# Four feed-forwards that open with two tiles of plain products, in a transformer program on one Trainium2 core

## The chip, the core and the metric

The program runs on one core of one Trainium2 chip. Times are device microseconds (us) of one execution. PE is TensorE (matmul), DVE VectorE, ACT ScalarE, POOL GpSimd, SP the engine that issues the loads.

## What is computed

Two blocks over 512 tokens of 1,024 channels, in float32. The first has two layers, each a feed-forward, a mixer (SSD and S5; then chunked attention and pooling) and another feed-forward; the second is a hybrid mixer and one feed-forward between layer norms. The five feed-forwards are called ffn0 to ffn4 here.

```python
def _swiglu(h, w_gate, w_up, w_down):
    return (jax.nn.silu(h @ w_gate) * (h @ w_up)) @ w_down
...
    for layer in range(DEPTH):
        h = _rmsnorm(x, ffn1_norm[layer])
        x = x + 0.5 * _swiglu(h, ffn1_w_gate[layer], ffn1_w_up[layer], ffn1_w_down[layer])
        h = _rmsnorm(x, mix_norm[layer])
...
        x = x + mixed.astype(x.dtype)
        h = _rmsnorm(x, ffn2_norm[layer])
        x = x + 0.5 * _swiglu(h, ffn2_w_gate[layer], ffn2_w_up[layer], ffn2_w_down[layer])
...
        x = layer_norm(alpha * x + mix, ln1_g[l], ln1_b[l])
        ff = swiglu_ffn(x, w_ffn_gate[l], w_ffn_up[l], w_ffn_down[l])
```

## The kernel before

x lies in SBUF with channels on partitions: eight tiles x[d] of 128 channels by 512 tokens, taken in the order DORD = 0, 4, 1, 5, 2, 6, 3, 7. A float32 operand is split in two parts of a type that PE takes at full rate: ACT copies the high part (xh, wh, th, aH), DVE subtracts it from the operand for the low part (xl, wl, tl, aL). A product of two operands is three matmuls: high by high, low by high, high by low.

A feed-forward has 2,816 = 22 tiles of 128 inner channels f, in parts of 7, 8 and 7. For each f gate and up are multiplied over the eight d, then silu and the product make a; after a part its down products add to x (stt, L280). ffn1 to ffn3 are normed: the gain is multiplied in with the split, and rstd (one over the root of the mean square) is multiplied in behind the products. rstd needs products with ones over the sums of squares (ssum, sq), a chain of operations on four columns on DVE (small), and a product with csts that spreads it over the partitions.

**Quad.** A tile f is done by `quad` (L512). Gate and up for two token halves and two halves of d would be eight block products; with sums of weights and sums of operands seven do. That is 7 × 4 × 3 = 84 matmuls of 256 columns. `wsums` (L572) makes the sums of weights sa and sb on POOL; `prep_t` (L457) makes the sums of operands: for k = 0 to 3, from x[k] and x[k+4], four differences (tt), and splits them into seven slots of th and tl. Four of the slots lie in the room of xh and xl, three in th1 and tl1.

In ffn1, ffn2 and ffn3 every tile is a quad, so `prep_t(k)` runs as soon as x[k] and x[k+4] are there: in `even` and `odd` (L971, L1362) behind the mixer's last products, in `epi_res` (L718) behind ffn1's down products. ffn0 opens with plain products: in part 0 each f is 48 matmuls of 512 columns, and its sums are made after that part.

**ffn4's opening.** The layer norm before it goes by token halves. `ahead` (in the main function) first issues the right half's sums; `quad_a` multiplies the two block products that need the left half alone, for four tiles; between them `ln_cols_b`, `ln_rows` and `ln_apply` (L1877, L1895, L1907) normalise the right half, and `prep_t1` makes the sums. `quad_b` does the other five block products of these tiles.

The tile scheduler orders each engine's instructions by priority; weight splits have `high_priority`, and inside `pe_order` PE keeps the order of the code. PSUM tiles are named by tags (mm, aux, acc, p12) with a number of buffers each. A load is 512 KB per gate or up weight, in five buffers `raw`.

Of the kernel before, what the change touches and what calls it, by code (L numbers as in the profile page):

```python
# [9 lines left out]
F32 = mybir.dt.float32  # L10
# [7 lines left out]
T = 512  # L18
# [20 lines left out]
T4 = 5  # L39
AHEAD = 4  # L40
# [210 lines left out]
class Net:  # L251
# [164 lines left out]
    def prep(self, k, gain, steps=3):  # L416
        x = self.x[:, k]
        if gain is None:
            self.hilo(self.xh[:, k], self.xl[:, k], x)
            return  # L420
        if steps & 1:
            gc = self.vec(gain, k)
            self.act(self.xh[:, k], x, AF.Copy, scale=gc)
            self.stt(self.xl[:, k], x, gc, self.xh[:, k].bitcast(F32), ALU.mult, ALU.subtract)
# [3 lines left out]
        self.act(sq, x, AF.Square)  # L428
# [11 lines left out]

    def t_open(self):
        self.tx = ExitStack()
        self.tpool = self.tx.enter_context(self.tc.tile_pool(name="tx", bufs=1, side="right", reuse_waits="tile"))
        b = lambda t: t.rearrange("p (s k) (u t) -> p (s k u t)", s=4, u=2).rearrange("p (s k t) -> p s k t", s=4, k=4)
        self.th0, self.tl0 = b(self.xh), b(self.xl)
        self.th1 = self.tpool.tile([128, 3, 4, H], F32R, name="th1")
        self.tl1 = self.tpool.tile([128, 3, 4, H], F32R, name="tl1")
        self.TH = [self.th0[:, s] for s in range(4)] + [self.th1[:, s] for s in range(3)]
        self.TL = [self.tl0[:, s] for s in range(4)] + [self.tl1[:, s] for s in range(3)]
# [7 lines left out]
    def prep_t(self, k, gain, stats=True):  # L457

        G = self.nc.gpsimd
# [17 lines left out]
        if gain is not None and stats:  # L477
            sq = self.t4([2, T], "sq2")
            self.act(sq[:, 0], self.x[:, k], AF.Square)
            self.act(sq[:, 1], self.x[:, k + 4], AF.Square)  # L480
            if k == 0:
                self.ssum = self.sp.tile([128, T], F32, name="ssum", tag="ssum", bufs=1)
                self.add(self.ssum, sq[:, 0], sq[:, 1], self.on("sst"))
            elif k < 3:
                self.add(self.ssum, self.ssum, sq[:, 0], self.on("sst"))
                self.add(self.ssum, self.ssum, sq[:, 1], self.on("sst"))
            else:
                self.sums = [self.ssum, sq[:, 0], sq[:, 1]]

    def prep_t0(self, d):  # L490

        if d == 0:
            b = lambda t: t.rearrange("p (s k) (u t) -> p (s k u t)", s=4, u=2).rearrange("p (s k t) -> p s k t", s=4, k=4)
            self.th0, self.tl0 = b(self.xh), b(self.xl)
        s, k = d // 4, d % 4
        self.hilo(self.th0[:, s, k], self.tl0[:, s, k], self.x[:, d, 0:H])

    def prep_t1(self, k):

        G = self.nc.gpsimd  # L500
# [34 lines left out]
    def quad_a(self, src):  # L535

        t = self.wp.tile([128, 8, 128], F32, name="raw", tag="raw", bufs=5)
        self.nc.sync.dma_start(t, src)
        with self.tc.high_priority(offset=PRIO):
            h, l = self.wsplit(t)  # L540
        ps = self.psum("p12")
        for k in range(4):
            for s in range(2):
                o = ps[:, H * s:H * s + H]
                j = 4 * s + k
                self.mm(o, h[:, j], self.TH[s][:, k], k + s == 0, False)
                self.mm(o, h[:, j], self.TL[s][:, k], False, False)
                self.mm(o, l[:, j], self.TH[s][:, k], False, k + s == 4)
        return ps

    def quad_b(self, sp, src1, src2, by_k):

        r = []
        for s in (src1, src2):
            t = self.wp.tile([128, 8, 128], F32, name="raw", tag="raw", bufs=5)
            self.nc.sync.dma_start(t, s)
            r.append(t)
        r1, r2 = r
        with self.tc.high_priority(offset=PRIO):
            wa, wb, w2 = self.wsums(sp, r1, r2)  # L560
# [1628 lines left out]
```

## Time and profile before

| | before |
|---|---|
| three runs | 2833.72, 2842.39, 2843.31 us; median 2842.39 |
| profiled execution | 2844.66 us; span 2842.9 us |
| busy: PE, DVE, ACT, POOL | 2747.3, 1921.9, 1608.5, 966.1 us |

Busy time is an average over stages with different limits. The timeline gives start, duration, engine, line, operation and tile, then the idle time before it and what released it; durations of neighbours overlap a little, since an engine starts on the next while the last result is written. f and d of a product are told by its place.

### The profile page before, as it was taken

How to read it: one execution, taken by the hardware profiler on the slowest of the kernel's cores; microseconds unless marked ns; L12 is line 12 of the kernel's file. 1: busy time of each engine (PE TensorE's matmuls, PEld its weight loads, DVE VectorE, ACT ScalarE, POOL GpSimd, SP SyncE). 2: the span in 40 equal slices, each digit the busy share in tenths (PEclk: the TensorE clock that was granted, in tenths of full speed). 3: DMA queues.
4: the chain of work that ended last, by engine and by line, in shares of the span. 5: the costliest groups of instructions: out<-in, count | busy, mean ns of one | idle time of the engine just before them, and what ended most of it. 6: DMA issues, size and time to landing. Idle time of an engine off the chain costs nothing. (4 is left out here: it accounts for less than half of the span.)

```text
span 2842.9 us, 44877 instructions
## 1 busy us (share of the span) xinstructions
PE 2747.3 (97%) x16940; PEld 2453.4 (86%) x16940; DVE 1921.9 (68%) x3472; ACT 1608.5 (57%) x2593; POOL 966.1 (34%) x849
## 2 busy tenths in 40 slices
PE   8899999989999999999998999999999999889997
PEld 6798988879999899998777999987888788889997
DVE  7885856688576886766556867675886434765665
ACT  5375834647676766766434767653443543466674
POOL 5752414235344353442002534421000102544352
PEclk9999998999999999999999999999999899899998
DMA  5333354203332233324221333234323133132321
GB/s 181 114 108 101 107 156 124 84 30 100 108 113 89 86 96 106 115 89 127 72 67 33 99 107 117 89 110 137 95 86 103 55 101 114 53 104 97 119 86 56
DMA packets 106760, 279.58 MB, mean 98 GB/s; under 512 B 31984, under 2 KB 34672, under 8 KB 106544
## 3 DMA queue, kind: packets, MB, share of 16 engines
q1 hardware_dynamic: 106400, 276.54, 31.2%
q8 instruction: 133, 2.18, 0.3%
q14 instruction: 83, 0.68, 0.1%
q10 hardware_dynamic: 144, 0.18, 0.0%
HBM read 258.54 MB, written 11.85 MB: 95 GB/s over the span
## 5 line engine op out<-in xcount | busy, mean ns | idle before, releaser
L290 ACT ACTIVATE wh<-raw 128x1024 fp32r<-128x1024 f32 (+2 forms) x467 | 439.0, 944 | 608.0 <-PE mm L293 456.9
L293 PE MATMUL mm<-xh,wh 128*128 128x512 f32 (+1 forms) x1592 | 556.4, 350 | 18.3 <-ACT wh L290 7.0
L293 PE MATMUL mm<-xh,wl 128*128 128x512 f32 (+1 forms) x1592 | 546.6, 343 | 4.9 <-DVE wl L265 4.9
L293 PE MATMUL mm<-xl,wh 128*128 128x512 f32 (+1 forms) x1592 | 547.2, 344 | 3.9 <-DVE xl L280 2.3
L265 DVE TENSOR_TENSOR wl<-raw,wcopy 128x512 fp32r<-128x512 f32 (+1 forms) x410 | 257.1, 659 | 212.4 <-PE mm L293 92.7
L293 PEld LDWEIGHTS mm<-xh,wh 128*128 128x128 f32 x1592 | 309.5, 194 | 59.7 <-issue 11.5
L265 POOL TENSOR_TENSOR sa<-raw 128x512 f32<-128x512 f32 x103 | 139.5, 1354 | 617.6 <-DVE wl L265 266.0
L293 PEld LDWEIGHTS mm<-xh,wl 128*128 128x128 f32 x1592 | 309.2, 194 | 39.7 <-DVE wl L265 6.2
L293 PEld LDWEIGHTS mm<-xl,wh 128*128 128x128 f32 x1592 | 309.4, 194 | 36.4 <-DVE xl L280 4.9
L265 DVE TENSOR_TENSOR wl<-raw,wh 128x1024 fp32r<-128x1024 f32 (+1 forms) x159 | 205.4, 1293 | 124.6 <-ACT wh L290 118.5
L293 PE MATMUL aux<-xh,wh 128*128 128x256 f32 (+1 forms) x880 | 262.3, 298 | 5.2 <-DVE x L265 3.3
L293 PE MATMUL aux<-xh,wl 128*128 128x256 f32 (+1 forms) x880 | 261.8, 297 | 2.9 <-DVE wl L265 2.9
L293 PE MATMUL aux<-xl,wh 128*128 128x256 f32 (+1 forms) x880 | 261.2, 297 | 3.2 <-DVE xl L265 3.2
L293 PE MATMUL mm<-th,wh 128*128 128x256 f32 x824 | 232.7, 282 | 5.1 <-DVE x L265 3.3
L290 ACT ACTIVATE wcopy<-raw 128x512 fp32r<-128x512 f32 (+1 forms) x410 | 229.2, 573 | 8.3 <-DVE wl L265 7.7
L293 PE MATMUL mm<-tl,wh 128*128 128x256 f32 x824 | 231.5, 281 | 0.3 <-DVE tl L265 0.2
L293 PE MATMUL mm<-th,wl 128*128 128x256 f32 x824 | 230.8, 280 | 0.0
L293 PEld LDWEIGHTS aux<-xh,wh 128*128 128x128 f32 x880 | 174.5, 198 | 8.4 <-DVE x L265 3.6
L293 PEld LDWEIGHTS aux<-xh,wl 128*128 128x128 f32 x880 | 173.8, 198 | 6.0 <-DVE wl L265 3.5
L293 PEld LDWEIGHTS aux<-xl,wh 128*128 128x128 f32 x880 | 173.5, 197 | 6.1 <-DVE xl L265 3.7
L265 DVE TENSOR_TENSOR wl<-sa,wcopy 128x512 fp32r<-128x512 f32 x186 | 126.3, 684 | 76.2 <-ACT wcopy L290 44.9
L265 POOL TENSOR_TENSOR wl<-raw,wh 128x512 fp32r<-128x512 f32 x103 | 140.4, 1363 | 108.9 <-ACT wh L290 108.9
(491 smaller groups left out, 7081.4 us busy)
## 6 DMA issues: line engine op xcount, KB each, us to landing
raw<-in_gu SPq DMA_DIRECT2D x224, 512.0 KB, 3.8
raw<-in_wd SPq DMA_DIRECT2D x80, 448.0 KB, 3.3
raw<-in_hy_in SPq DMA_DIRECT2D x60, 512.0 KB, 3.8
raw<-in_wd SPq DMA_DIRECT2D x40, 512.0 KB, 3.5
raw<-in_ev_in SPq DMA_DIRECT2D x17, 512.0 KB, 3.9
raw<-in_od_in SPq DMA_DIRECT2D x16, 512.0 KB, 3.8
sw<-qk SPq DMA_DIRECT2D x48, 128.0 KB, 2.3
raw<-in_ev_out SPq DMA_DIRECT2D x8, 512.0 KB, 3.8
```

The lines of the kernel that those rows point to most:

```text
L265: (eng or self.nc.vector).tensor_tensor(out=out, in0=a, in1=b, op=op)
L290: self.nc.scalar.activation(out, a, func, **kw)
L293: self.nc.tensor.matmul(ps, a, b, start=start, stop=stop)
```

## The change

- **ffn1, ffn2, ffn3** (`open_plain`): f = 0 and 1 are plain products, 48 matmuls of 512 columns each. Tile 0 has d outside and gate and up inside, tile 1 gate then up. The sums of squares come after tile 0, the spread of rstd after tile 1's gate. `prep_t` is called after tile 0's products.
- **ffn4** (`open_halves`): f = 0 and 1 by token halves, four PSUM tiles at once for the left half, then three for the right and the fourth behind: 96 matmuls of 256 columns a tile. The layer norm of the right half comes as hooks between the left half's d; `prep_u` splits one d of one half.
- xh and xl are now written at once in the quad's slots (`slot`), by `prep(..., slots=True)`, so the plain products read them in two pieces of 256 columns (`direct`), in ffn0's part 0 too. `prep_t` makes the four sums alone; th1 and tl1 hold four slots, not three; the buffers t4 are 3, not 5.
- `quad_a`, `quad_b`, `prep_t0` and `prep_t1` go. Squares are summed on POOL to two tensors, not three, before the products with ones.

```diff
-T4 = 5
-AHEAD = 4
+T4 = 3
+ND = 2
...
-        self.th1 = self.tpool.tile([128, 3, 4, H], F32R, name="th1")
+        self.th1 = self.tpool.tile([128, 4, 4, H], F32R, name="th1")
...
+    def slot(self, t, d):
+
+        q = self.quarters(t)
+        return q[:, 0:4:3, d] if d < 4 else q[:, 1:3, d - 4]
...
         tt = self.t4([4, H], "tt")
-        self.hilo(self.th0[:, 0, k], self.tl0[:, 0, k], aL)
         self.sub(tt[:, 0], aR, aL)
-        self.hilo(self.th0[:, 3, k], self.tl0[:, 3, k], tt[:, 0])
-        self.hilo(self.th0[:, 1:3, k], self.tl0[:, 1:3, k], b.rearrange("p (u t) -> p u t", u=2))
+        self.sub(tt[:, 2], bR, aR, self.on("tt"))
         self.sub(tt[:, 1], bR, tt[:, 0])
-        self.sub(tt[:, 2], bR, aR, self.on("tt"))
         self.sub(tt[:, 3], bL, tt[:, 1])
-        self.hilo(self.th1[:, :, k], self.tl1[:, :, k], tt[:, 1:4])
...
+        self.hilo(self.th1[:, :, k], self.tl1[:, :, k], tt)
...
+    def direct(self, ps, w, d, lo=0, hi=2):
+
+        o = ps if hi - lo == 2 else ps[:, H * lo:H * hi]
+        ah, al = self.slot(self.xh, d)[:, lo:hi], self.slot(self.xl, d)[:, lo:hi]
+        h, l = w
+        self.mm(o, h[:, d], ah, d == DORD[0], False)
+        self.mm(o, h[:, d], al, False, False)
+        self.mm(o, l[:, d], ah, False, d == DORD[7])
...
+    def open_plain(self, i, gain):
+
+        A = self.A
+        out = []
+        with self.pe_order():
+            for f in range(ND):
+                w = [self.weights(A["gu"][i, f, :, s]) for s in range(2)]
+                ps = [self.psum("mm"), self.psum("aux")]
+                for d, s in ([(d, s) for d in DORD for s in range(2)] if f == 0 else [(d, s) for s in range(2) for d in DORD]):
+                    self.direct(ps[s], w[s], d)
+                    if f == 1 and d == DORD[7] and s == 0:
+                        self.rms_b("acc")
+                if f == 0:
+                    self.rms_a("acc")
+                out.append(ps)
+                if f == 0:
+                    for k in range(4):
+                        self.prep_t(k, gain)
+        return out
+
+    def open_halves(self, i, hooks):
+
+        A = self.A
+        with self.pe_order():
+            hooks[-1]()
+            w = [self.weights(A["gu"][i, f, :, s]) for f in range(2) for s in range(2)]
+            ps = [self.psum(t) for t in ("mm", "aux") * 2]
+            for n, d in enumerate(DORD):
+                for t in range(4):
+                    self.direct(ps[t], w[t], d, 0, 1)
+                if n in hooks:
+                    hooks[n]()
+            for d in DORD:
+                for t in range(3):
+                    self.direct(ps[t], w[t], d, 1, 2)
+            for d in DORD:
+                self.direct(ps[3], w[3], d, 1, 2)
+        for k in range(4):
+            self.prep_t(k, None)
+        return [ps[0:2], ps[2:4]]
...
-            if last and not ffn_next:
-                self.prep(d, gain)
-            elif last and d >= 4:
-                self.prep_t(d - 4, gain)
+            if last:
+                self.prep(d, gain, slots=ffn_next)
...
-            self.prep_t(d2, gain)
+                self.prep(d, gain, slots=True)
...
+            hooks = {-1: lambda: self.ln_cols_a(1, "acc"), 1: cols, 5: rows}
+            self.ffn(4, None, epi, tail=self.ln_tail, hooks=hooks)
```

**DVE ahead of and in ffn3's opening.** x_72 is x; the additions of mm_ tiles are those of the mixer's last products, and the twelfth row is that of x[7]. Before, x[6] and x[3] are added in the first and the seventh row:

```order
L265 TENSOR_TENSOR x_72<-x_72,mm_16206 128x512
L265 TENSOR_TENSOR xl_74<-xg_16165,xh_73 128x2x256
L265 TENSOR_TENSOR tt_16223<-xg_16220 128x256
L265 TENSOR_TENSOR tl1_16075<-tt_16168,th1_16074 128x3x256
L265 TENSOR_TENSOR xl_74<-xg_16220,xh_73 128x256
L265 TENSOR_TENSOR tt_16223<-xg_16220,tt_16223 128x256
L265 TENSOR_TENSOR x_72<-x_72,mm_16247 128x512
L265 TENSOR_TENSOR tt_16223<-xg_16220,tt_16223 128x256
L265 TENSOR_TENSOR xl_74<-tt_16223,xh_73 128x256
L265 TENSOR_TENSOR xl_74<-xg_16220,xh_73 128x2x256
L265 TENSOR_TENSOR tt_16278<-xg_16275 128x256
L265 TENSOR_TENSOR x_72<-x_72,mm_16261 128x512
```

Of the change, the twelve rows up to x[7], with x[6] and x[3] in the fourth and the ninth; wl_16004 is the split of tile 0's up weight, wl_16124 that of tile 1's gate weight:

```order
L265 TENSOR_TENSOR wl_16004<-raw_16001,wh_16003 128x1024
L280 SCALAR_TENSOR_TENSOR xl_74<-x_72,vecs_75,xh_73 128x2x256
L265 TENSOR_TENSOR tt_16094<-xg_16091,tt_16094 128x256
L265 TENSOR_TENSOR x_72<-x_72,mm_15918 128x512
L265 TENSOR_TENSOR tl1_15985<-tt_16084,th1_15984 128x4x256
L265 TENSOR_TENSOR tt_16094<-xg_16091,tt_16094 128x256
L280 SCALAR_TENSOR_TENSOR xl_74<-x_72,vecs_75,xh_73 128x2x256
L265 TENSOR_TENSOR wl_16124<-raw_16121,wh_16123 128x1024
L265 TENSOR_TENSOR x_72<-x_72,mm_15943 128x512
L280 SCALAR_TENSOR_TENSOR xl_74<-x_72,vecs_75,xh_73 128x2x256
L265 TENSOR_TENSOR tt_16104<-xg_16101 128x256
L265 TENSOR_TENSOR x_72<-x_72,mm_15962 128x512
```

The quarter-wide xl of the sums are gone; whole xl (128x2x256), splits of both tiles' weights and the four-wide tl1 stand between the additions now, and xl of d = 3 and 7 still come behind x[7].

**PE at the start of ffn3.** Before, with mm_16261 the last product of the mixer:

```order
L293 MATMUL mm_16261<-yl_14490,wh_16243 128x512
L293 MATMUL mm_16261<-yh_14489,wl_16244 128x512
L293 MATMUL mm_16328<-xh_73,wh_16306 128x256
L293 MATMUL mm_16328<-xl_74,wh_16306 128x256
L293 MATMUL mm_16328<-xh_73,wl_16307 128x256
```

Of the change, with mm_15962 that last product, and mm_16007 and aux_16008 the gate and up tiles of f = 0:

```order
L293 MATMUL mm_15962<-yh_14223,wl_15940 128x512
L293 MATMUL mm_16007<-xh_73,wh_15997 128x512
L293 MATMUL mm_16007<-xl_74,wh_15997 128x512
L293 MATMUL mm_16007<-xh_73,wl_15998 128x512
L293 MATMUL aux_16008<-xh_73,wh_16003 128x512
L293 MATMUL aux_16008<-xl_74,wh_16003 128x512
L293 MATMUL aux_16008<-xh_73,wl_16004 128x512
L293 MATMUL mm_16007<-xh_73,wh_15997 128x512
```

The first products of 256 columns read one slot and one weight; now three of 512 for gate are followed at once by three for up. The PSUM buffer of aux_16008 is that of mm_15962, which the addition of x[7] reads.

**DVE at the end of ffn4's opening.** Before, from the last two tl1 on (pu is the first step of tile 0's sums):

```order
L265 TENSOR_TENSOR tl1_24553<-tt_24707,th1_24552 128x3x256
L265 TENSOR_TENSOR tl1_24553<-tt_24724,th1_24552 128x3x256
L265 TENSOR_TENSOR pu_24797<-pu_24797,mm_24822 128x256
L265 TENSOR_TENSOR wl_24916<-sb_24906,wh_24915 128x1024
L265 TENSOR_TENSOR pu_24797<-pu_24797,mm_24822 128x256
L265 TENSOR_TENSOR aux_24821<-pu_24797,aux_24821 128x256
L265 TENSOR_TENSOR acc_24823<-pu_24797 128x256
```

Of the change, from the last two xl on; aux_24203 and aux_24205 are f = 0's and f = 1's up tiles, wl_24528 is f = 2's:

```order
L265 TENSOR_TENSOR xl_74<-x_72,xh_73 128x256 x2
L265 TENSOR_TENSOR tt_24498<-x_72,tt_24498 128x256
L265 TENSOR_TENSOR tl1_24163<-tt_24491,th1_24162 128x4x256
L265 TENSOR_TENSOR tt_24498<-x_72,tt_24498 128x256
L265 TENSOR_TENSOR aux_24203<-aux_24203,u_24505 128x512
L265 TENSOR_TENSOR aux_24205<-aux_24205,u_24512 128x512
L265 TENSOR_TENSOR tl1_24163<-tt_24498,th1_24162 128x4x256
L265 TENSOR_TENSOR aL_24509<-aux_24203,aH_24508 128x512
L265 TENSOR_TENSOR aL_24516<-aux_24205,aH_24515 128x512
L265 TENSOR_TENSOR wl_24528<-raw_24523,wcopy_24530 128x512
L265 TENSOR_TENSOR wl_24528<-raw_24523,wcopy_24533 128x512
```

The last sums stand behind the last xl, and f = 2's weight split behind the epilogues of both plain tiles and the last tl1.

## Rows read from the trace of the kernel before

**Rows 1.** The page, parts 1 and 2: PE's total, and its clock by slice.

```profile
PE 2747.3 (97%) x16940; PEld 2453.4 (86%) x16940; DVE 1921.9 (68%) x3472; ACT 1608.5 (57%) x2593; POOL 966.1 (34%) x849
...
PEclk9999998999999999999999999999999899899998
```

**Rows 2.** Windows (stretch; length, busy us by engine, clock, DMA, GB/s): four openings, steady state.

```profile
625.95:664.57 38.62, 30.57 (x198) 29.50 (x196) 35.56 (x47) 22.65 (x35) 27.15 (x19) 0.78 0.21 68
984.45:1020.55 36.10, 31.55 (x198) 30.90 (x197) 28.48 (x42) 18.95 (x29) 22.26 (x16) 0.76 0.24 74
1549.00:1587.55 38.55, 31.29 (x198) 30.48 (x198) 34.09 (x46) 20.80 (x31) 26.76 (x18) 0.73 0.17 55
2445.70:2530.30 84.60, 64.89 (x442) 61.65 (x441) 64.03 (x120) 45.22 (x76) 47.12 (x38) 0.84 0.21 68
2600.00:2660.00 60.00, 60.00 (x506) 60.00 (x505) 45.77 (x84) 48.81 (x78) 36.46 (x30) 1.00 0.33 107
```

**Rows 3.** The chain that ended last (start, us, what): two quads, ffn4.

```profile
2651.50 5.71 PE mm L293 x48
...
2661.51 5.71 PE mm L293 x48
```

**Rows 4.** Waits of PE in 1549 to 1588: total us, times, longest.

```profile
PE mm L293 <- DVE x L265: 3.6, 1, 3.6
PE aux L293 <- DVE x L265: 3.3, 1, 3.3
```

**Rows 5.** Waits of PE in 2445 to 2531, ffn4's opening.

```profile
PE mm L293 <- DVE x L265: 3.3, 1, 3.3
PE aux L293 <- DVE xl L265: 3.2, 2, 2.0
```

**Rows 6.** Windows: from the first to the last addition before ffn3.

```profile
1534.52:1557.90 23.38, 17.18 (x74) 13.84 (x72) 23.38 (x29) 15.47 (x28) 15.06 (x11) 0.87 0.00 0
```

**Rows 7.** Timeline of DVE (start, us, operation) ahead of ffn3: additions to x.

```profile
1534.52 1.89 DVE L265 TENSOR_TENSOR x<-x,mm 128x512 f32<-128x512 f32 x3 [0.82 <-PE mm L293]
...
1557.90 0.68 DVE L265 TENSOR_TENSOR x<-x,mm 128x512 f32<-128x512 f32 x1
```

**Rows 8.** Timeline of DVE, ffn1's opening: split, xl, x[7], scalars of rstd.

```profile
613.24 1.22 DVE L265 TENSOR_TENSOR wl<-raw,wh 128x1024 fp32r<-128x1024 f32 x1
...
630.32 1.49 DVE L265 TENSOR_TENSOR xl<-tt,xh 128x256 fp32r<-128x256 f32 x1
...
634.82 0.68 DVE L265 TENSOR_TENSOR x<-x,mm 128x512 f32<-128x512 f32 x1
...
641.64 0.16 DVE L287 TENSOR_SCALAR small<-aux 128x4 f32<-128x4 f32 x1 [0.27 <-PE aux L293]
...
649.29 1.41 DVE L280 SCALAR_TENSOR_TENSOR small<-small 128x4 f32<-128x4 f32 x2
```

**Rows 9.** Timeline of DVE, ffn4's opening: the last xl.

```profile
2480.69 0.41 DVE L265 TENSOR_TENSOR xl<-tt,xh 128x256 fp32r<-128x256 f32 x1
```

**Rows 10.** Timeline of POOL beside the xl at 630.32.

```profile
630.07 1.45 POOL L265 TENSOR_TENSOR sa<-raw 128x512 f32<-128x512 f32 x1
```

**Rows 11.** Timeline of PE in ffn0's plain products, the first and the last of 19.

```profile
59.76 0.39 PE L293 MATMUL aux<-xl,wh 128*128 128x512 f32 x1
...
63.84 0.39 PE L293 MATMUL aux<-xl,wh 128*128 128x512 f32 x1
```

**Rows 12.** Timeline of PE in ffn1's opening, two products of 256 columns.

```profile
632.07 0.41 PE L293 MATMUL aux<-xh,wh 128*128 128x256 f32 x1
632.28 0.41 PE L293 MATMUL aux<-xl,wh 128*128 128x256 f32 x1
```

**Rows 13.** Timeline of PE, ffn4: a wait, and the first product of f=5.

```profile
2518.65 0.58 PE L293 MATMUL mm<-xh,wl 128*128 128x256 f32 x1 [2.66 <-DVE wl L265]
...
2530.30 0.28 PE L293 MATMUL aux<-xh,wh 128*128 128x256 f32 x1
```

More of the change, by code (lines that the diff above doesn't have):

```diff
@@ L477, in prep_t @@
[L477 to L488, printed above, removed]
@@ L591, in wsplit, with rms_a, rms_b @@
         return h, l
-    def rms_a(self):
+    def rms_a(self, tag="aux"):
         v = self.small(4)
-        self.ts(v, self.col_sums([self.sums]), 1.0 / 1024, EPS, ALU.mult, ALU.add)
+        self.ts(v, self.col_sums([self.sums], tag=tag), 1.0 / 1024, EPS, ALU.mult, ALU.add)
         self.rstd_c = self.rsqrt(v, 4)
-    def rms_b(self):
+    def rms_b(self, tag="aux"):
         self.rstd = self.sp.tile([128, T], F32, name="rstd", tag="rstd", bufs=1)
-        self.act(self.rstd, self.rows(self.rstd_c), AF.Copy, scale=RS)
+        self.act(self.rstd, self.rows(self.rstd_c, tag), AF.Copy, scale=RS)
     def rms(self):
@@ L604, in rms @@
         self.rstd_rows([self.sums], 1.0 / 1024, EPS, self.rstd)
-    def ffn(self, i, normed, epi, bg=None, first=None, tail=None, ahead=None):
+    def open_plain(self, i, gain):
[16 more added lines that the diff above has]
+        return out
@@ L608, in ffn @@
+    def ffn(self, i, gain, epi, bg=None, tail=None, hooks=None):
         nc, A = self.nc, self.A
         G = nc.gpsimd
-        if ahead:
-            self.spare = 0
-            self.psum_open(p12=AHEAD, aux=2, mm=1, acc=1)
-        elif not first:
-            self.lend()
-        with self.tc.tile_pool(name="ffn", bufs=1, reuse_waits="tile") as fp:
-            pend = []
-            if ahead:
-                order = self.pe_order()
-                order.__enter__()
-                ahead(-1)
-                for f in range(AHEAD):
-                    pend.append(self.quad_a(A["gu"][i, f, :, 0]))
-                    ahead(f)
+        first = bg is not None
+        normed = gain is not None
+        if not first:
+            self.t_open()
+            if hooks:
+                self.spare = 0
+                self.psum_open(mm=2, aux=2, acc=4)
+            else:
+                self.lend()
+        with self.tc.tile_pool(name="ffn", bufs=1, reuse_waits="tile") as fp:
+            if not first:
+                plain = self.open_halves(i, hooks) if hooks else self.open_plain(i, gain)
@@ L626, in ffn @@
                 for f in range(f0, f0 + nf):
-                    if ahead and f == AHEAD:
-                        order.__exit__(None, None, None)
+                    if hooks and f == ND:
                         self.lend()
@@ L631, in ffn @@
                         self.spare = 2 if f >= NDIR else 1
-                    if first and part == 0:
-                        ps = []
-                        for s in range(2):
-                            w = self.weights(A["gu"][i, f, :, s] if f + s else None)
-                            p = self.psum("mm" if s == 0 else F0T)
-                            self.mm3(p, w, 0, 8, self.xh, self.xl)
-                            ps.append(p)
-                        if f == 0:
-                            self.rms()
+                    if first and part == 0 or f < ND:
+                        if first:
+                            ps = []
+                            for s in range(2):
+                                w = self.weights(A["gu"][i, f, :, s] if f + s else None)
+                                ps.append(self.psum("mm" if s == 0 else F0T))
+                                for d in DORD:
+                                    self.direct(ps[s], w, d)
+                            if f == 0:
+                                self.rms()
+                        else:
+                            ps = plain[f]
```

182 lines of the change are left out of this document (59 added, 123 removed).

## The prediction

> **What bounds the kernel now.** I read the page first: TensorE (PE) is busy for 97% of the span and its clock is at or near full in nearly every slice [rows 1]. So the end is set by PE's own work and by the few places where PE stands. The windows over the four openings of ffn1, ffn2, ffn3 and ffn4, each from PE's first product of the feed-forward to the first of a later tile, come second [rows 2]. The stretch 2600 to 2660 is the steady state: PE busy for all of 60.00 us at clock 1.00. The openings are not like that. In 38.62, 36.10 and 38.55 us PE does two tiles in ffn1, ffn2, ffn3, and in 84.60 us five tiles in ffn4, at a mean clock of 0.73 to 0.84, which lies between the two levels of 1.2 and 2.4 GHz. A steady tile takes 10.01 us, from 2651.50 to 2661.51 in the chain [rows 3]. Two would be 20.0 us and five 50.1. So the openings hold 18.6 + 16.1 + 18.5 + 34.5 = 87.7 us over steady work: all that any change to them can win.
>
> Third, who is waited for. In ffn3's opening PE waits for DVE's additions to x, 3.6 and 3.3 us [rows 4]; in ffn4's for additions to x and for xl [rows 5]. In the 23.38 us that end at the last addition before ffn3, DVE is busy for 23.38 us [rows 6]: there DVE is the bound, not PE.
>
> **How DVE spends that time.** The stretch holds seven additions of 512 columns (0.63 us each, a third of 1.89 [rows 7]), one split of 1,024 (1.22 [rows 8]), 16 operations on 256 columns (0.41 when alone [rows 9]), three of 512 (0.63) and two of 768 (about 0.9, between 0.63 and 1.22): 4.4 + 1.2 + 6.6 + 1.9 + 1.8 = 15.9 us. The other 7.5 us are DVE held: an xl of 256 columns that starts at 630.32, beside POOL's sa (630.07, 1.45 us), takes 1.49 us [rows 8, 10]. POOL was busy for 15.06 us of the stretch [rows 6], so about half of its time held DVE.
>
> The Trainium skill, SBUF — State Buffer, section Who interferes with whom, says that a DVE instruction with two SBUF inputs and a GpSimd instruction that reads SBUF exclude each other for the whole instruction. By that rule the two engines' times would add in full, 15.9 + 15.1 = 31.0 us where the trace shows 23.38; the trace agrees with the mechanism (1.49 for 0.41) and bears out half of its size.
>
> **The change, part by part.**
>
> *Products.* A plain tile is 48 products of 512 columns; 18 of them take 63.84 − 59.76 = 4.08 us [rows 11], so 0.2267 each, 10.88 us a tile: 0.87 more than a steady tile. Six such tiles add 5.2 us. A tile by halves is 96 products of 256 columns at 10.01/84 = 0.119 us: 11.4 us, 1.4 more; two add 2.8. So 8.0 us of PE work are added and must be paid from the stands. Fewer sums over squares are priced at nothing. The plain products read xh and xl in two pieces of 256 columns, which no row shows for them; the least is 0, the most that each costs as two products of 256, 0.238 − 0.227 = 0.012 us, times 624 (336 of them in ffn0) = 7 us. I take 0, since a quad's products of 256 columns run at nearly the same rate per column.
>
> *ffn2.* Its x comes from ffn1's down products, 21 of 0.2267 = 4.76 us for each d. Between two of them DVE has one addition and one xl (0.63 each), half a set of sums (three or four of 0.41 in two), half of tl1 (0.61) and a down split (1.2): under 4.1 us. DVE keeps up, so the products run: 21.8 us for two tiles, about 1 for the sums of squares, then the stand for rstd. Those scalars took from 641.64 to 650.70, 9.1 us [rows 8], and now only tile 1's 24 gate products (5.4 us) cover them: up to 3.5 us. Together 26 against 36.10: **10 us won**; 12 if the scalars are quicker, 6 if the stand costs clock too.
>
> *ffn3.* The order shows what stands ahead of the last x. Up to the addition of x[7] DVE now has seven additions (4.4), three splits (3.7; two more than before), six xl of 512 (3.8), seven sums of 256 (2.9) and one tl1 of 1,024 (1.2): 16.0 us, against 15.9. Held as before, x[7] ends where it did, 1558.58, that is 9.6 us after the opening [rows 7]. PE's second product group, aux, uses the PSUM bank that this addition frees, and with both weights inside the loop over d it comes fourth. So PE stands from 0.7 to 9.6 us here too. Then come 45 products (10.2), 1 us of sums, tile 1 (10.9), the stand of up to 3.5, and what half clock costs (a product of 256 columns takes 0.21 us at 632.07 [rows 12], so it doubles the time; I take 3): 38.2 against 38.55. **0 won**; 6 if the scalars are covered and the clock recovers at once, −4 if x[7] comes 4 us later.
>
> *ffn1.* The DVE order is the same and x[7] at 634.82 was 8.9 us after the opening too [rows 8], but aux needs only weights here. PE runs the d whose xl are done and waits for xl of d=3 and 7, which stand behind x[7], tl1, a sum and a split: about 14.5 us after the opening. Then 12 products (2.7), 1, 10.9, 3.5 and 3 for half clock: 35.6 to 37.6, as that xl comes at 14.5 or 16.5. Against 38.62 **2.5 won** (−3 to 8).
>
> *ffn4.* The left-half tiles replace products that ran there before. The right half needs the same normalised x as before; the last xl ended at 2481.10 [rows 9]. After it come 18 products and 24 more (5.0 us at 0.119), then on DVE a multiplication, tl1, two aL and two splits ahead of f=2's rest (0.63 + 1.2 + 1.3 + 1.3 = 4.5): 2490.6. What follows such a split took 2530.30 − 2518.65 = 11.65 us [rows 13], then two quads of 10.01: 2522.3 against 2530.30. **8 won**. Its ends: 14, if xl comes early; 0, if the four wider tl1 (0.3 each) and the sums among xl put it off by 4 us and f=3 waits as well.
>
> *ffn0* loses nothing: its sums are made under part 0's down products as before. DMA bytes are the same.
>
> Sum: 2.5 + 10 + 0 + 8 = 20.5 us less. The profiled execution took 2844.66 us, so 2824.2; it is 2.3 above the median of 2842.39, which gives **2822**.
>
> **The rivals.**
>
> *A, no stands:* DVE and POOL keep up everywhere. The three openings would take 21.8 + 1 + 1.5 = 24.3 us: 14.3 + 11.8 + 14.3 won, and 12 in ffn4: 52 us, 2790. For it: the sums are no longer needed by the first products. Against it: the order puts them ahead of the last xl on a DVE that is busy for all of [rows 6].
>
> *B, the change doesn't make its sums under the plain products but before them:* then only ffn2, whose x comes slowly, wins 10; ffn1 loses 3, ffn3 is even and ffn4 is even: 7 us less, 2835, within 0.5%. For it: tt, tl1 and three splits stand between the additions to x in ffn1 and ffn3.
>
> *C, slower, by DVE held longer:* three splits and six wide xl each take two SBUF inputs while POOL sums squares and makes sa and sb. If the two engines' times add in full, 16.0 + 15.1 = 31.1 us from 1534.52, x[7] ends 17.3 us into ffn3, not 9.6, and ffn1's xl comes as much later. The openings are then 45.9 and 43.3 us: 7.3 + 4.7 lost; ffn4's chain of x and xl, slowed alike, loses 8, and ffn2 at 4.1 us of 4.76 has no reserve left and wins nothing: 20 us, 2862. It decides from x[7] ending 10 us after the opening, where ffn3 is even. Against it: only half of POOL's time held DVE in [rows 6]. Here stands the skill's rule of above; it would give this case.
>
> **How the numbers follow.** A measurement of this kernel can tell about 0.5%, 14 us. Forecast 0.50 (2808 to 2832; a tenth of it less than 14 us won), A 0.13, B 0.25, C 0.12. Faster by over 0.5%: 0.45 + 0.13 = 0.58; within: 0.05 + 0.25 = 0.30; slower: 0.12. The range leaves out half of A and most of C: 2796 to 2846, which takes in 7 us for two-piece operands on the forecast and on B.
>
> **What would show it.** ffn2's opening to f=2 near 26 us with no stand over 4 us. In ffn3 a stand of some 9 us after three products, released by DVE's x; in ffn1 one or two shorter ones by xl. A stand before the broadcast of rstd (csts) in tile 1. In ffn4 f=5 some 8 us nearer to the last product of the mixer. Plain products at 0.227 us. The prediction is wrong if ffn1 and ffn3 open in under 30 us (A), or if x[7] ends later than 10 us into them (C).

## The result and the profile after

| | before | after |
|---|---|---|
| median of four runs (lowest to highest) | 2842.85 us (2833.72 to 2843.95) | 2806.94 us (2801.28 to 2811.16) |
| profiled execution: time, span | 2844.66, 2842.9 us | 2808.35, 2806.6 us |

The ratio is 0.9879, with a 95% interval of 0.9852 to 0.9907: 1.2% faster, 36 us where 20.5 were forecast. 2806.94 lies inside the range of 2796 to 2846, but just below the forecast's own 2808 to 2832: in the part of the range that was put there for rival A and not for the forecast.

The page of the changed kernel, parts 1 and 2, answers to [rows 1]:

```profile
PE 2726.1 (97%) x16724; PEld 2420.9 (86%) x16724; DVE 1879.3 (67%) x3398; ACT 1597.7 (57%) x2553; POOL 917.0 (33%) x808
...
PEclk9999998999999999999999999999999899999998
```

PE is busy for 21.2 us less although some 8 us of products were forecast to be added: products at half clock count as busy twice as long, and there are fewer of them (mean granted clock of the execution 0.977, before 0.968). POOL's work shrank by 49.1 us, DVE's by 42.6.

The windows over the four openings, up to PE's first product of f = 2 (of f = 5 in ffn4), answer to [rows 2] (length, busy us of PE, PEld, DVE, ACT, POOL, clock, DMA, GB/s). In ffn1 and ffn2 they start at PE's first product of the feed-forward. In ffn3 and ffn4 they start at the end of the mixer's last product, here and in [rows 2], which the prediction calls the first product of the feed-forward: that one comes 6.9 us (before: 3.8) and 2.9 us (before: 2.9) later, so these two windows hold the first stand as well.

```profile
624.09:656.12 32.03, 26.02 (x117) 21.07 (x116) 28.50 (x39) 21.09 (x30) 18.92 (x13) 0.95 0.16 51
975.51:1001.10 25.59, 24.61 (x118) 20.04 (x116) 22.50 (x32) 16.35 (x24) 15.35 (x10) 1.00 0.19 64
1530.68:1566.90 36.22, 28.00 (x118) 22.52 (x117) 28.30 (x39) 20.99 (x30) 19.15 (x13) 0.81 0.14 45
2421.66:2494.17 72.51, 61.80 (x467) 59.79 (x466) 51.63 (x112) 47.50 (x78) 32.52 (x24) 0.93 0.16 50
```

Against before that is 6.6 + 10.5 + 2.3 + 12.1 = 31.5 us of the span's 36.3. Most of it is clock. PE's idle time in these rows is 39.6 us before and 25.9 now, while length × (1 − clock), with the clock as a share of its upper level, an estimate of what the lower level takes from PE, is 8.5 + 8.7 + 10.4 + 13.5 = 41.1 us before and 1.6 + 0 + 6.9 + 5.1 = 13.6 now. So 13.7 us of stands and about 27 us of clock were won, against the 8 us of added products. This is read from the rows; no run sets the clock by itself.

The other 4.8 are spread over the rest, in pieces of under 3.5 us either way, in stages that the change hardly touches. The start of ffn1 alone lay anywhere from 620.8 to 630.7 us in eleven runs of the variants below, whose code up to there differs little, so these 4.8 aren't told apart from differences between runs.

Now the stands, by opening. PE in ffn1 (timeline: start, duration, operation, then the idle time before it and what released it):

```profile
638.95 0.79 PE L293 MATMUL mm<-xl,wh 128*128 128x512 f32 x1 [5.19 <-DVE xl L280]
...
641.25 0.63 PE L293 MATMUL mm<-xh,wh 128*128 128x512 f32 x1
641.68 0.51 PE L293 MATMUL mm<-xl,wh 128*128 128x512 f32 x1
...
642.94 0.28 PE L293 MATMUL acc<-ones,ssum 128*128 128x1 f32 x2
...
644.64 0.48 PE L293 MATMUL mm<-xh,wh 128*128 128x512 f32 x1
...
648.17 0.39 PE L293 MATMUL mm<-xh,wh 128*128 128x512 f32 x1
...
649.99 0.39 PE L293 MATMUL mm<-xh,wl 128*128 128x512 f32 x1
650.21 0.60 PE L296 MATMUL acc<-csts,small 128*128 128x128 f32 x4
```

The stand for xl of d = 3 ends 14.9 us after the opening (14.5 forecast for the last xl; that of d = 7 is written 15.8 us in and holds nothing). For 2.7 us the clock is at its lower level (1.2 GHz, 0.43 us from product to product), then at the upper one (2.4 GHz). The sums of squares take 1.70 us, and the spread of rstd (csts) follows the gate products with no stand at all, where 3.5 us were allowed for. From 648.17 to 649.99 eight products take 1.82, 0.2275 each against 0.2267 in [rows 11]: reading xh and xl in two pieces costs nothing that can be seen.

DVE at that place, the scalars of rstd, answer to the last two rows of [rows 8]:

```profile
645.29 0.15 DVE L287 TENSOR_SCALAR small<-acc 128x4 f32<-128x4 f32 x1
...
647.10 1.33 DVE L280 SCALAR_TENSOR_TENSOR small<-small 128x4 f32<-128x4 f32 x2
...
648.66 0.36 DVE L280 SCALAR_TENSOR_TENSOR small<-small 128x4 f32<-128x4 f32 x2
```

They are done by 649.02, 3.7 us after their start, where [rows 8] had 9.1. The windows over the scalars, before and after; POOL's load is the last busy time:

```profile
641.64:650.70 9.06, 9.06 (x57) 9.06 (x58) 8.88 (x13) 2.71 (x4) 7.20 (x5) 0.70 0.16 55
```
```profile
645.29:649.02 3.73, 3.73 (x18) 3.07 (x17) 3.52 (x12) 1.92 (x4) 1.28 (x1) 1.00 0.44 141
```

PE in ffn3, and the addition that it waits for on DVE, answer to [rows 4] and [rows 7]:

```profile
1537.59 0.76 PE L293 MATMUL mm<-xh,wh 128*128 128x512 f32 x1 [6.75 <-DVE x L265]
...
1540.68 0.76 PE L293 MATMUL aux<-xh,wh 128*128 128x512 f32 x1 [1.47 <-DVE x L265]
...
1546.36 0.44 PE L293 MATMUL aux<-xl,wh 128*128 128x512 f32 x1
...
1560.99 0.60 PE L296 MATMUL acc<-csts,small 128*128 128x128 f32 x4
```
```profile
1535.11 1.75 DVE L265 TENSOR_TENSOR wl<-raw,wh 128x1024 fp32r<-128x1024 f32 x1
1536.77 0.67 DVE L265 TENSOR_TENSOR x<-x,mm 128x512 f32<-128x512 f32 x1
...
1539.86 0.68 DVE L265 TENSOR_TENSOR x<-x,mm 128x512 f32<-128x512 f32 x1
```

x[7] is there 9.9 us after the opening (9.6 forecast). One thing was read wrongly: the first product already stands, for x[3], since mm's PSUM buffer is freed by that addition. The three gate products therefore come late rather than at once; the price is the same, as aux stands until x[7] in any case. Half clock lasts until 1546.4, and csts doesn't stand here either.

ffn2 has one stand of 0.85 us, ahead of csts, and runs at full clock throughout.

ffn4, DVE from the first apply of the layer norm on the right half to the last xl, answers to [rows 9]; the windows behind it give POOL's load beside that stretch, before and after:

```profile
2437.24 0.87 DVE L280 SCALAR_TENSOR_TENSOR x<-x,vecs,acc 128x256 f32<-128x256 f32 x2 [5.46 <-ACT acc L290]
...
2451.21 0.75 DVE L265 TENSOR_TENSOR xl<-x,xh 128x256 fp32r<-128x256 f32 x2
```

Window of the kernel before, from the same apply to its last xl:

```profile
2462.46:2481.10 18.64, 11.98 (x69) 10.92 (x68) 18.61 (x34) 10.05 (x21) 10.91 (x12) 0.68 0.18 58
```

And of the changed kernel:

```profile
2437.24:2451.96 14.72, 10.34 (x65) 9.34 (x64) 14.72 (x37) 8.76 (x17) 4.73 (x4) 0.88 0.01 2
```

DVE is busy throughout in both, with 34 and 37 operations, but needs 14.7 us instead of 18.6, while POOL is busy for 4.73 instead of 10.91. The last xl ends 30.3 us after the opening; before it was 35.4.

### The profile page after: what moved, and what is told of

The parts are those of the page before. It is cut to its first block, busy times and chain, and to the rows that moved or that the text cites. A ratio compares the mean times of both kernels' runs of the same rounds, so it can differ in the third digit from the quotient of the medians.

```text
span 2806.6 us, 44257 instructions
## 1 busy us (share of the span) xinstructions
PE 2726.1 (97%) x16724; PEld 2420.9 (86%) x16724; DVE 1879.3 (67%) x3398; ACT 1597.7 (57%) x2553; POOL 917.0 (33%) x808
## 5 line engine op out<-in xcount | busy, mean ns | idle before, releaser
L293 PE MATMUL mm<-xh,wh 128*128 128x512 f32 (+1 forms) x1260 | 465.6, 369 | 16.9 <-ACT wh L290 7.0
L293 PE MATMUL mm<-xl,wh 128*128 128x512 f32 (+1 forms) x1260 | 455.9, 362 | 11.3 <-DVE xl L280 8.3
L293 PE MATMUL mm<-xh,wl 128*128 128x512 f32 (+1 forms) x1260 | 454.9, 361 | 2.4 <-DVE wl L265 2.4
L293 PE MATMUL mm<-th,wh 128*128 128x256 f32 x1140 | 319.7, 280 | 0.8 <-ACT wh L290 0.8
L293 PE MATMUL mm<-tl,wh 128*128 128x256 f32 x1140 | 318.2, 279 | 0.0
L293 PE MATMUL mm<-th,wl 128*128 128x256 f32 x1140 | 318.2, 279 | 0.0
L293 PEld LDWEIGHTS mm<-xh,wh 128*128 128x128 f32 x1260 | 243.3, 193 | 59.9 <-issue 15.0
L293 PEld LDWEIGHTS mm<-xl,wh 128*128 128x128 f32 x1260 | 243.5, 193 | 46.1 <-DVE xl L280 11.3
L293 PEld LDWEIGHTS mm<-th,wh 128*128 128x128 f32 x1140 | 214.7, 188 | 1.0 <-ACT wh L290 1.0
L293 PEld LDWEIGHTS mm<-th,wl 128*128 128x128 f32 x1140 | 214.4, 188 | 0.0
L293 PEld LDWEIGHTS mm<-tl,wh 128*128 128x128 f32 x1140 | 214.0, 188 | 0.0
```

The lines of the kernel that those rows point to most:

```text
L293: self.nc.tensor.matmul(ps, a, b, start=start, stop=stop)
```

## The experiments

All are edits of the changed kernel. The number that they are read by is the time of a stage: from where the opening's window starts to the first down product of the feed-forward, in us, from the trace. The expectations call that start PE's first product.

| | ffn1 | ffn2 | ffn3 | ffn4 | time |
|---|---|---|---|---|---|
| before | 88.63 | 86.11 | 88.56 | 104.60 | 2844.66 |
| the change | 81.93 | 75.50 | 86.12 | 92.46 | 2808.35 |
| the change, again | 82.29 | 75.48 | 84.76 | 94.16 | 2807.51 |
| sums behind the last xl | 85.02 | 75.50 | 83.86 | 92.39 | 2809.21 |
| quads open ffn1, ffn3 | 89.72 | 75.48 | 88.03 | 93.12 | 2818.19 |
| quads open ffn2, ffn4 | 81.88 | 81.65 | 84.84 | 105.10 | 2828.54 |
| no sums of squares on POOL | 75.88 | 75.50 | 80.96 | 93.17 | 2799.51 |
| sums in two lots | 82.04 | 75.46 | 81.08 | 95.94 | 2803.58 |
| layer norm earlier | 82.12 | 75.48 | 86.19 | 90.69 | 2803.30 |
| both of these | 80.56 | 76.00 | 81.07 | 90.62 | 2796.51 |
| both, rstd spread earlier | 85.12 | 74.64 | 84.48 | 90.54 | 2812.32 |
| POOL kept busy in ffn4 | 82.00 | 75.48 | 86.06 | 97.33 | 2817.81 |
| POOL kept busy beside the scalars | 84.95 | 75.47 | 87.28 | 95.96 | 2815.56 |

Times are of the profiled executions, one for each row. Stages with the same code differ by 0.4 us in ffn1, 1.4 in ffn3 and 3.6 in ffn4 (92.39 to 95.96), so in one run smaller differences say nothing. In ffn4 the difference is clock: PE stands for 10.0 to 10.6 us in each of these seven runs, but the lower level lasts for 10.2 us of the stage in the two shortest and for 20.5 in the two longest.

**The sums behind the last xl.** In ffn1 and ffn3 the operands' sums take their gain from a tensor that needs the last xl, so none stands ahead of it on DVE.

```diff
...
+ z, gv = self.small(1), self.small(8)
+ self.ts(z, self.slot(self.xl, 7)[:, 1, H - 1:H].bitcast(F32), 0.0, None, ALU.mult)
+ self.ts(gv, self.vec(gain, 0, 8), z, None, ALU.add)
...
- self.prep_t(k, gain)
+ self.prep_t(k, gain, gv)
```

> Edit: in ffn1 and ffn3 the sums of operands (tt, tl1) can't start before the last xl is written; all else as in the change. Theory (the sums stand on DVE ahead of the last additions to x and the last xl, and are held there by POOL): without them DVE has 12 us of work, not 16, ahead of x[7], and half as many operations that POOL can hold; x[7] ends 1 to 4 us into ffn3 instead of 10.0. From PE's first product to f=2, ffn1 goes from 32.0 to 26 us (25 to 28) and ffn3 from 36.2 to 27 (25 to 29); the whole takes about 2792 us. Rival 1 (the weight splits and POOL's sums of squares make DVE late, not the sums of operands): ffn1 stays over 30 and ffn3 over 34. Rival 2 (the sums are needed at f=2 and come late there): f=2 starts earlier, but PE then stands for tl1 or tt in f=2 and f=3 starts where it did; the whole stays near 2807.

The stands in tile 0 went as the theory has it: none in ffn1, 0.94 and 1.21 us in ffn3. But a new one came, ahead of the spread of rstd; here in ffn1 and in ffn3:

```profile
653.89 1.11 PE L296 MATMUL acc<-csts,small 128*128 128x128 f32 x4 [8.09 <-DVE small L280]
...
1560.36 0.65 PE L296 MATMUL acc<-csts,small 128*128 128x128 f32 x4 [3.87 <-DVE small L280]
```

The late sums now lie among the scalars. ffn1 loses 2.7 to 3.1, ffn3 wins 0.9 to 2.3. Neither theory nor rival had this wait, which is the one that the prediction had priced at 3.5.

**Quads open ffn1 and ffn3 again**, behind the change's own sums.

```diff
+ if i in (1, 3) and not hooks:
+     plain = []
+     for k in range(4):
+         self.prep_t(k, gain)
+ else:
      plain = self.open_halves(i, hooks) if hooks else self.open_plain(i, gain)
...
+ if f == 0 and normed:
+     self.rms()
...
```

> Edit: ffn1 and ffn3 open with quads for f=0 and 1 again (sums of operands first, rstd behind f=0's quad), with the new layout of the sums. Theory (each opening's gain is its own): ffn1's opening goes back from 32.0 to about 38.5, ffn3's from 36.2 to about 38.5, the whole to about 2816; ffn2 and ffn4 stay at 25.6 and 72.5. Rival (the gain of ffn1 and ffn3 comes from the leaner sums, four slots split at once, and not from plain products): ffn1 stays within 1.5 us of 32 and ffn3 of 36.

Both go back to where they were before (89.72 for 88.63, 88.03 for 88.56). So the gain in these two is that of the plain tiles; the leaner sums give nothing there.

**Quads open ffn2; ffn4 opens with the old block products.**

```diff
+ if hooks:
...
+     for f in range(4):
+         pend.append(self.quad_a(A["gu"][i, f, :, 0]))
+         hooks(f)
+ elif i == 2:
+     plain = []
+     for k in range(4):
+         self.prep_t(k, gain)
+ else:
+     plain = self.open_plain(i, gain)
...
- hooks = {-1: lambda: self.ln_cols_a(1, "acc"), 1: cols, 5: rows}
- self.ffn(4, None, epi, tail=self.ln_tail, hooks=hooks)
+ self.ffn(4, None, epi, tail=self.ln_tail, hooks=ahead)
```

> Edit: ffn2 opens with quads for f=0 and 1 again, ffn4 with two block products of four tiles ahead and the rest of each quad behind the layer norm, as before the change, with the new layout of the sums. Theory: ffn2's opening goes back from 25.6 to about 36, ffn4's (to f=5) from 72.5 to about 84; ffn1 and ffn3 stay at 32.0 and 36.2; the whole takes about 2829 us. Rival (in ffn4 the leaner sums and the layer norm's modes made the gain): ffn4 stays under 78.

ffn4 is back (105.10). ffn2 goes only to 81.65: of its 10.6 us the plain tiles give 6.2, and 4.5 stay with quads. The change also made the sums and the sums of squares leaner and calls them at another place; that these give the 4.5 us is likely, but no run takes them back by themselves.

**No sums of squares on POOL in ffn1 and ffn3.**

```diff
- self.add(self.ssum, t, sq, self.on("ssum"))
+ if gain in ("ffn2_0", "ffn2_1"):
+     self.ssum = t
+ else:
+     self.add(self.ssum, t, sq, self.on("ssum"))
```

> Edit: in ffn1 and ffn3 the squares of x are not summed over the eight d (POOL's additions to ssum go, some 8 us of POOL in each opening; the mean square is then taken from the first and the last d alone). Theory (POOL holds DVE's operations with two SBUF inputs for about half of its own time): x[7] ends some 4 us earlier in ffn3, 6 instead of 10.0 us into it; the openings go to about 28 (ffn1) and 32 (ffn3). Rival 1 (the two exclude each other in full): x[7] ends 8 us earlier, and ffn3 opens in about 28. Rival 2 (DVE is late by its own work): no change, 32.0 and 36.2.

In ffn3 x[7] ends at 1529.91 with the opening at 1524.44: 5.5 us in, instead of 9.9 (theory: 6). DVE's timeline, first and last of the additions to x:

```profile
1509.98 1.88 DVE L265 TENSOR_TENSOR x<-x,mm 128x512 f32<-128x512 f32 x3 [0.82 <-PE mm L293]
...
1529.23 0.68 DVE L265 TENSOR_TENSOR x<-x,mm 128x512 f32<-128x512 f32 x1
```

From the first to the last of these additions DVE runs 25 operations here and in the change, but POOL is busy for 8.75 us instead of 16.40, and DVE takes 19.25 us instead of 23.67. The stages win 6.1 to 6.4 (ffn1) and 3.8 to 5.2 (ffn3). So of POOL's 7.7 us 4.4 held DVE, somewhat over half.

**The sums in two lots**: k = 0 and 1 behind the last xl, k = 2 and 3 behind the scalars of rstd.

```diff
+ if gv is not None and k == 2:
+     z, gv = self.small(1), self.small(8)
+     self.ts(z, self.rstd_c[:, 0:1], 0.0, None, ALU.mult)
+     self.ts(gv, self.vec(gain, 0, 8), z, None, ALU.add)
  self.prep_t(k, gain, gv)
```

> Edit: as in the run with late sums, but the sums for k=0 and 1 wait for the last xl and those for k=2 and 3 for the scalars of rstd. Theory (in that run the scalars waited on DVE behind the late sums, which made PE stand 8.09 us in ffn1 and 3.87 in ffn3 before rstd is spread): with two of four sums behind the scalars that stand is under 1 us in both. From PE's first product to the first down product, ffn1 takes 75 us (74 to 77; the change 81.93, late sums 85.02) and ffn3 78 (76 to 80; 86.12 and 83.86). Rival (the sums for k=2 and 3 now come too late for f=2, whose products need all four): a stand for tl or tt in f=2 of 3 us or more, ffn1 over 79, ffn3 over 82.

ffn3 wins 3.7 to 5.0, between theory and rival. ffn1 wins nothing. There tile 0 has no stand any more, so PE's sums of squares end at 635.51; but the two early sums and two weight splits stand ahead of the scalars on DVE, whose first starts at 639.70. PE then stands ahead of csts, and at f = 2 for 0.84 and 0.69 us besides:

```profile
643.61 0.78 PE L296 MATMUL acc<-csts,small 128*128 128x128 f32 x4 [2.49 <-DVE small L280]
```

**The layer norm earlier**: ffn4's apply comes behind the fourth d of the left half, not the sixth.

```diff
- hooks = {-1: lambda: self.ln_cols_a(1, "acc"), 1: cols, 5: rows}
+ hooks = {-1: lambda: self.ln_cols_a(1, "acc"), 1: cols, 3: rows}
```

> Edit: in ffn4's opening the spread of the layer norm's scalars comes after the fourth d of the left half, not the sixth. Theory (in the change the scalars were ready 3.1 us before PE came to the spread, 2431.78 against 2434.91, and the right half's chain on DVE sets the end of the opening): the chain starts 2.9 us earlier and ffn4 to the first down product takes 90 us (89 to 91) instead of 92.46. Rival (PE's own work sets the end, and PE only changes the order of its products): 92.5, with the products of the left half's last d filling no stand.

90.69 as expected. With this edit ffn4 took 90.54 to 90.69 in three runs, without it 92.39 to 95.96 in seven. Part of that is clock: where the lower level lasts for the same 10.2 us, it is 90.62 and 90.69 with the edit against 92.39 and 92.46 without, 1.8 us.

**Both of these edits**, the late sums in two lots and the earlier layer norm, run five times, with the change itself beside it:

> Edit: the two edits before in one kernel. Theory: the gains add, 7 + 8 + 2.5 us less than the change, about 2789 us where the change takes 2807. Rival: one of the two fails as its own run shows, 2797 to 2805.

> Edit: none, the change once more, on the chip of this call. Theory: 2807 us, ffn1 81.9, ffn2 75.5, ffn3 between 84.8 and 86.1, ffn4 92.5 from PE's first product to the first down product. It is what the other three are compared with.

Both edits: 2796.83 us (2792.69 to 2801.84, five runs), ratio to before 0.9836 [0.9818, 0.9853]. The change: 2809.85 (2807.51 to 2812.07, four runs), 0.9881 [0.9865, 0.9896]. The intervals don't overlap, and 13 us are won over the change; of the 11.0 between the two profiled runs the four stages hold 8.4. The theory's 2789 is missed by 8 us, and 2797 is where the rival begins: of the theory's 7 + 8 + 2.5 us the stages of ffn1, ffn3 and ffn4 show 1.7 + 3.7 + 3.5, the last of them partly clock. This is the fastest version in this study.

**Both, and rstd spread earlier**: csts behind the fifth d of tile 1's up products rather than behind the gate.

```diff
- if f == 1 and d == DORD[7] and s == 0:
+ if f == 1 and d == DORD[4] and s == 1:
```

> Edit: late sums and the earlier spread of ffn4, as together before, and in ffn1 to ffn3 the spread of rstd comes after the fifth d of tile 1's up products, not after its gate products. Theory (PE's stand of 2.5 us before the spread in ffn1 costs its length and some 2 us of half clock behind it): the stand goes, ffn1 to the first down product takes 77 us instead of 80.6 to 82, ffn2 75 and ffn3 81; the whole 2793 us where the two edits together took 2796.8. Rival (the epilogue of tile 0 then comes 3.4 us later and f=2 stands for its PSUM buffer as long): no change within 1.5 us.

It failed: 2812.05 us (2807.35 to 2812.82), 0.9882 [0.9866, 0.9899]. The stand ahead of csts is gone, and a longer one takes its place at f = 2, for the high part of its weights, which ACT copies behind the late sums' th and rstd. PE in ffn1, and the window behind the first stand:

```profile
660.41 0.58 PE L293 MATMUL acc<-th,wh 128*128 128x256 f32 x1 [5.45 <-ACT wh L290]
...
663.80 0.58 PE L293 MATMUL acc<-th,wl 128*128 128x256 f32 x1 [2.59 <-POOL wl L265]
```
```profile
661.00:670.00 9.00, 6.41 (x33) 6.20 (x33) 6.51 (x9) 3.02 (x5) 2.75 (x2) 0.56 0.17 58
```

PE got to f = 2 sooner than f = 2's operands did. PE now stands for 8.0 us in ffn1, where both edits alone leave it 4.0, and the clock is at its lower level for 10.2 us (0.56 over the 9 us of this window) instead of 3.4.

**POOL kept busy in ffn4**: twelve additions of 256 columns, whose results nothing reads, beside the right half's apply.

```diff
+ for _ in range(3):
+     scr = self.sp.tile([128, T], F32, name="sq", tag="sq", bufs=2)
+     self.add(scr[:, 0:H], self.x[:, k, H:T], self.x[:, k + 4, H:T], self.nc.gpsimd)
```

> Edit: the change with twelve additions of 256 columns more on POOL (three for each of the four steps that normalise the right half in ffn4's opening, about 0.75 us each when alone); their results aren't used, DVE's order is that of the change. Theory (ffn4 won more than forecast since POOL, which made sums of weights there before, stands idle beside the right half's chain on DVE and holds none of it): about half of the added 9 us holds DVE again, so from the first normalising operation to the last xl of the opening it takes 18 to 20 us instead of 14.7 (18.6 before the change), and ffn4 to the first down product 96 to 98 us. Rival (the chain is faster by its own order of operations): 14.7 stays, ffn4 92.5 to 94.2.

DVE's operations are the same 37 as in the change's window above, but they take as long as the 34 of the kernel before:

```profile
2442.82:2461.50 18.68, 10.90 (x67) 9.70 (x66) 18.68 (x37) 8.95 (x17) 11.96 (x13) 0.82 0.01 1
```

POOL 11.96 us busy instead of 4.73 makes 18.68 of 14.72. In the ten runs that open ffn4 by halves without the filler the stretch takes 14.71 to 14.73. ffn4 takes 97.33.

**POOL kept busy beside the scalars** of rstd in ffn1 and ffn3:

```diff
+ scr = self.sp.tile([128, T], F32, name="sq", tag="sq", bufs=2)
+ self.add(scr[:, 0:4], v, v, self.nc.gpsimd)
+ for _ in range(5):
+     self.add(scr, self.x[:, 0], self.x[:, 4], self.nc.gpsimd)
```

> In the change POOL does one addition of 1.28 us beside the scalars of rstd, which take 3.7 us (645.29 to 649.02 in ffn1), where before five of POOL's operations stood beside them and they took 9.1. Here POOL makes five additions of 512 columns (about 1.3 us each, 6.4 us) right behind the first scalar in ffn1 and ffn3, into a tensor that nothing reads. Theory, that POOL's quiet made the scalars short: half of POOL's 6.4 us is added to them or more, 3.7 becomes 7 to 9 us, and PE stands 1 to 4 us ahead of the spread of rstd (csts), where it did not stand. Rival, that it was DVE's own splits of weights between the scalars that went: the scalars take 3.7 to 4.5 us and PE does not stand ahead of csts. Either way f=2's weight sums on POOL come about 6 us later, and may cost a stand of their own at f=2, which is not counted here.

The scalars take 7.8 us, from 645.75 to 653.56 (3.7 in the change), and PE stands again, 2.82 us in ffn1 and 2.33 in ffn3. DVE, POOL and PE in ffn1:

```profile
645.75 0.15 DVE L287 TENSOR_SCALAR small<-acc 128x4 f32<-128x4 f32 x1
...
646.51 1.14 DVE L287 TENSOR_SCALAR small<-small 128x4 int32<-128x4 int32 x1
...
652.25 1.31 DVE L280 SCALAR_TENSOR_TENSOR small<-small 128x4 f32<-128x4 f32 x2
```
```profile
646.33 1.29 POOL L265 TENSOR_TENSOR sq<-x 128x512 f32<-128x512 f32 x1
```
```profile
653.62 0.65 PE L296 MATMUL acc<-csts,small 128*128 128x128 f32 x4 [2.82 <-DVE small L280]
```

The order on DVE is that of the change, two weight splits among the scalars. POOL is busy for 6.57 us beside them instead of 1.28. Five of the nine scalars take 1.11 to 1.28 us, and each of the five ends within 0.03 us of one of POOL's additions. So the theory holds, with 7.8 in its 7 to 9 us: POOL's quiet made the scalars short. The rival has a part as well. Before, three splits of 1,024 columns stood among the scalars and took 3.4 us from start to start; now two of 512 take 1.2. Of the 5.3 us that the scalars lost, 2.2 are DVE's own splits, and the other 3.1 are put down to POOL.

## Why the prediction was right, and where its terms were off

**Direction and place: right; the size was too small in three openings of four, always the same way.** The openings were the place to win, and 31.5 of 36.3 us were won there, where 20.5 were forecast. That the time still lies in the range is luck in part: the range was drawn down to 2796 for half of rival A, whose mechanism is seen in ffn2 alone. Undoing the plain tiles pair by pair gives the openings back, except for a part of ffn2.

**ffn2, 10 forecast, 10.5 measured.** The sum was made from the products' own rate. Its closeness is partly two errors that cancel: the stand for rstd was 0.85 where 3.5 were allowed, and tile 0, the sums of squares, the gate, the spread and the up products took 11.3 + 1.7 + 5.7 + 6.0 us, 2.0 more than forecast. The gain isn't due to plain products alone, as the text reads: 4.5 us of it stay when quads open ffn2.

**ffn1, 2.5 forecast, 6.6 measured.** (The forecast's own 35.6 to 37.6 us would be 3.0 to 1.0 won.) The stand for xl was right (14.9 for 14.5), with 11 products behind it, not 12. Two terms were too large: the stand for rstd, 3.5, was 0, and half clock, 3, was 1.4: six products in the 2.73 us from 638.95 to 641.68 instead of 1.36. The sums of squares took 1.7 instead of 1. By the rows above, 14.86 to the end of that stand, 3.99 for the eleven products, 1.70, 5.57 for the gate and 5.91 for the spread and the up products are the window's 32.03.

**ffn3, 0 forecast, 2.3 measured.** x[7] came at 9.9 for 9.6, half clock cost 2.7 for 3 (13 products in the 5.68 us from 1540.68 to 1546.36 instead of 2.95), and the stand for rstd was again 0 instead of 3.5; the rest, sums of squares, spread and tile 1, took 1.3 more than allowed.

**The step that failed in both is the 9.1 us of [rows 8]** that were carried over as the price of the scalars. That row was right, and it described the scalars beside a POOL that was busy for 7.20 of 9.06 us, with three weight splits of 1,024 columns among them. The change moves the work beside them: POOL makes one sum there now, two splits of 512 are left, and they take 3.7. Keeping POOL busy there brings 7.8 back. The row's price belonged to the place, not to the operations.

**ffn4, 8 forecast, 12.1 measured.** What follows the last xl was forecast at 41.2 us and took 42.2. The last xl was taken to come 35.4 us after the opening, as before, and came at 30.3: 5.1 − 1.0 = 4.1 us more. The prediction looked for what the four wider tl1 would add on DVE and found that it might be later; it didn't see what POOL no longer does in that stretch: sums and a split of weights, and the last pair of the layer norm's applies, which DVE makes now. Of the 5.1 the chain from the first apply gives 3.9; with POOL's time filled again, it takes the 18.7 us of before. The other 1.2 is its earlier start, 15.6 us after the opening instead of 16.8, and that goes with the clock: in the other runs of the same code it starts 15.6 to 17.9 us in, later the longer the clock was low ahead of it. So 12.1 is the upper end of what this code gave: the stage is 8.6 to 12.2 us under the one run of before.

**Two-piece operands** at 0 were right, **rival A** (no stands, 24.3 us each) comes near in ffn2 alone (25.6), and **rival C** fell: no opening lost, and x[7] ended 9.9 us into ffn3 and 9.98 into ffn1, barely ahead of the 10 from which it was to decide. Of **rival B** the mechanism is there, since sums do stand ahead of the last xl in ffn1 and ffn3: taking them away ends the stands in tile 0. Its conclusion is not, as both still won.

The Trainium skill, SBUF — State Buffer, section Who interferes with whom, has a DVE instruction with two SBUF inputs and a GpSimd instruction that reads SBUF exclude each other for the whole instruction. The runs agree for single instructions: with POOL kept busy beside the scalars, an operation on four columns with two SBUF inputs took 1.28 us instead of 0.16 and ended 0.02 us after POOL's sum.

The prediction found that half of this rule's size is borne out. That half is a ratio of recorded times and doesn't weigh against the rule. POOL's records stretch beside DVE too: the same addition of the filler took 0.72 to 3.61 us. DVE's overlap their neighbours: from start to start the 29 operations of [rows 6] come to about 14.2 us when none is held, not 15.9. And in the filler's stretch 16 of DVE's 37 operations take an operand from PSUM; these stayed at 0.41 to 0.49 us. So the 4.0 us that 7.2 more of POOL's recorded time cost are a price for this mix of operations, not the size of a rule.

**Why two lots of sums win in ffn3 and not in ffn1:** in ffn3 tile 0 keeps stands of 0.96 and 1.20 us, so the scalars are ready before PE comes to csts; in ffn1 it keeps none, and PE stands there instead. In all PE's stands fall from 8.2 to 4.2 us in ffn3, but only from 6.0 to 4.0 in ffn1. And in that run the clock was at its lower level for 6.8 us of ffn1; with both edits, where it was so for 3.4 as in the change, the same code wins 1.4 us.

**Left open:** the 4.8 us outside the openings, and what gives the 4.5 us of ffn2 that stay with quads.

## What to carry to other kernels

A duration read from a trace holds for the company it was read in. Where a change moves work on POOL, price DVE's chains anew beside it, the shortest operations above all, and try first to keep POOL quiet beside the scalars or the additions that PE waits for. Where several chains share DVE ahead of a stand, each move of one uncovers the next (here xl, then rstd, then the weights of f = 2), so look for the order that spreads them, and measure two moves together before a third is made.

## What was not expected of the hardware

How unevenly POOL's work falls on DVE. In the changed kernel's stretch of 23.67 us ahead of ffn3, every addition x<-x,mm, whose second operand lies in PSUM, took 0.67 to 0.69 us however busy POOL was. Operations with both operands in SBUF took up to 1.1 us longer: xl of 512 columns 0.74 to 1.76, a sum of 256 columns 0.41 to 1.51, a split of 1,024 columns 1.22 to 2.32:

```profile
1525.45 2.32 DVE L265 TENSOR_TENSOR wl<-raw,wh 128x1024 fp32r<-128x1024 f32 x1
1527.69 0.74 DVE L280 SCALAR_TENSOR_TENSOR xl<-x,vecs,xh 128x512 fp32r<-128x512 f32 x1
1528.36 1.51 DVE L265 TENSOR_TENSOR tt<-xg,tt 128x256 f32<-128x256 f32 x1
1529.79 0.67 DVE L265 TENSOR_TENSOR x<-x,mm 128x512 f32<-128x512 f32 x1
```

So a chain of short operations pays most: each of them can wait for a whole operation of POOL, which makes a scalar of 0.16 us cost seven times as much, as five of nine did in the last run above.
